# Two VectorE sums kept in PSUM: the state's sum and the product of kappa write over their own input

## The chip, the cores and the metric

The program runs on one core of one Trainium2 chip. The metric is the device time of one execution in microseconds (us); the time of a kernel is the median of its runs. Engines are named as in the profile: PE is TensorE, DVE is VectorE, ACT is ScalarE, POOL is GpSimd, SP issues most DMAs.

## The reference

One block of a network on 512 tokens of width 1024: a normed input goes through one wide projection; its columns feed a convolution branch (31 taps), an RWKV-7 branch with a state per head, and two gates; the branches are merged, projected, and a feed-forward network follows.

```
u = h @ w_in
u_conv, u_rwkv, u_gate = jnp.split(u, [2 * CONV_DIM, 2 * CONV_DIM + RWKV_COLS], axis=-1)
...
kk = (k * k_k).reshape(hs)
kk = kk / jnp.maximum(jnp.linalg.norm(kk, axis=-1, keepdims=True), 1e-12)
...
def step(S, inp):
    r_t, w_t, k_t, v_t, a_t, b_t = inp          # a_t = -kk
    Sa = jnp.einsum('bhij,bhj->bhi', S, a_t)
    S = S * w_t[:, :, None, :] + Sa[..., None] * b_t[:, :, None, :] + v_t[..., None] * k_t[:, :, None, :]
    y = jnp.einsum('bhij,bhj->bhi', S, r_t)
    return S, y
```

## The kernel before

Channels lie on the 128 partitions, the 512 tokens along the free axis. Every large product is cut into **dense blocks** of 128 output columns: `wload` fetches 128x8x128 weights (one DMA on SP's queue, two buffers "raw"), ACT rounds them to `wH` (L215), POOL computes the rest `wL = raw - wH` (L216), and `wmul` issues 24 matmuls of 128x512 (L223, L224, L225 in turn, eight times) into one of three PSUM buffers "mm". 52 such blocks stand ahead of the second half of group 3's solve, where they fill TensorE between the small products; behind the recurrence come dense blocks almost alone.

The RWKV heads are worked off in four **groups** g = 0 to 3 of four heads (two blocks b of 128 channels). The state's recurrence is cut into eight chunks of 64 tokens. For each group:

- `group_k` and `group_prep`: keys, decays and the factors of the chunks. In its part `decay_k`, once for each block, so 8 times, `bcast_rows` spreads the inverse norms over a PSUM tile `prn`; L628 multiplies it into BK, L630 makes `kkn = k * k_k * prn` and L631 makes AR from kkn and the decays `Pt`. `prn` is one of two PSUM buffers "misc", which the tiles post, g, bonus, mean and sW take in turn.
- `group_solve`: a triangular system, 31 steps on VectorE (L722 and L724 in each) between two transposes (L715 at the start, L730 at the end); `group_solve2` is its second half on TensorE and begins with the products sW (L748).
- `group_chain`: the eight chunks one after the other. A chunk's products go through one PSUM buffer "ch" on TensorE (L768 and L770, L777, L785); the new state is `S = (pn + S) * PC`, in L792 and L793 (L789 where there is no state yet, once in each group). The next chunk's L768 reads S. L792 and L793 are executed 24 times, six in each group.
- `group_post`: for each of the two blocks a transposition on TensorE (L830, tile post), its eviction on DVE (L831), a product g (L835) with weights `g2t` fetched on SP into one buffer, and its eviction (L836). `group_bonus` gives one more small product and its eviction (L702) to each block. These belong to group g and are laid among the work of g + 1.

The convolution's taps (L145, VectorE, `acc` in PSUM, which is written over) fill VectorE between the steps of the chain. In group 3 the convolution's norm is laid in: a product mean (L893) on TensorE, eight subtractions on POOL (L903), squares on ACT (L905), their sums (L188), a root (L198), its reciprocal on DVE (L199) and its broadcast on TensorE (tile rmsb, L183).

The order on each engine isn't written out: the program's text gives every instruction a priority, shifted by the numbers in the table `FORWARD` (`forward("chain", g)` and so on) and by `amid` and `issue_after`, and a scheduler takes at each point the instruction whose buffers and inputs it holds to be ready by its own costs. Which buffers a line uses is therefore part of what sets the order of all lines behind it.

Of the kernel before, what the change touches and what calls it, by code (L numbers as in the profile page):

```python
# [10 lines left out]
ALU = mybir.AluOpType  # L11
# [3 lines left out]
P = 128  # L15
# [3 lines left out]
C = 64  # L19
# [38 lines left out]
def tile_block(ctx: ExitStack, tc: tile.TileContext, xT, vec, cst, x0, w_ada, w_in, w2a2, g2w,  # L58
# [5 lines left out]
    dve, act, pool, pe = nc.vector, nc.scalar, nc.gpsimd, nc.tensor  # L64
    cnt = [0]

    def nm(s):
        cnt[0] += 1
        return f"{s}{cnt[0]}"
# [17 lines left out]
    def t2k(shape=(P, T), dt=F32, tag="t2k", bufs=9):  # L87
        home = sb if tag == "t2k" else pools["A2" if tag in A2 else "A"]
        return home.tile(list(shape), dt, name=nm(tag), tag=tag, bufs=bufs)
# [10 lines left out]
    def pmisc(shape=(P, T), name="misc"):  # L100
        return psum("misc", 2, shape, name)
# [4 lines left out]
    def V(name, j=0, w=1):  # L106
        o = VEC[name][0] + j
        return vt[:, o:o + w]
# [72 lines left out]
    def bcast_rows(dst, rows):  # L181
        for q in range(4):
            pe.matmul(dst[:, q * P:(q + 1) * P], e4[:, q, :], rows, start=True, stop=True)  # L183
# [49 lines left out]
    def after_dense():  # L233

        return tc.issue_after(last[0].ins)

    @contextmanager
    def amid(n, d=-1):

        with forward("amid", shift=False), tc.issue_after(dense_log[d][n].ins):  # L240
            yield
# [17 lines left out]
    def w_in_block(c0):  # L259
        return dense(w_in, 0, c0, hH, hL)  # L260

    def shifted(acc, dst, j, ahead=0):
        act.activation(dst, acc, AF.Copy, scale=mix1[:, j:j + 1])
        with forward("shift") if ahead else ExitStack():
            dve.scalar_tensor_tensor(dst[:, 1:T], acc[:, 0:T - 1], V("mix", j), dst[:, 1:T], ALU.mult, ALU.add)
# [268 lines left out]
    NB = 2  # L534
# [3 lines left out]
    def r3(ap):  # L538
        return ap.rearrange("p (c t) -> p c t", t=C)

    def atile(tag, shape, bufs=1):
        return pools["A2" if tag in A2 else "A"].tile(list(shape), F32, name=nm(tag), tag=tag, bufs=bufs)
# [50 lines left out]
    def group_prep(g, G):  # L593
        blocks = [g * NB + b for b in range(NB)]
        G.AR = atile("AR", (P, NB, NCH, 2 * C))
        G.UV = atile("UV", (P, NB, NCH, 2, C))
        G.bkT = atile("bkT", (P, NB, NCH, 2, C))
        G.G = atile("G", (P, NB, 2, NCH, P))
        G.PC = atile("PC", (P, NB, NCH), 2)
        Pts, Pis, BKs, kps = [], [], [], []  # L600
        for b, p in enumerate(blocks):
            cum = G.sg[b]
            dve.tensor_tensor_scan(cum, cmask, cum, 0.0, ALU.mult, ALU.add)
            Pt = atile("Pt", (P, NCH, C + 1), 2)
            pool.memset(Pt[:, :, 0:1], 1.0)
            with tc.issue_after(G.sqrt.ins):
                act.activation(Pt[:, :, 1:], r3(cum), AF.Exp, scale=-KAPPA)
            pool.tensor_copy(G.PC[:, b, :], Pt[:, :, C])
            Pi = t2k()
            with tc.issue_after(G.sqrt.ins):  # L610
                act.activation(Pi, cum, AF.Exp, scale=KAPPA)
            Pts.append(Pt)
            Pis.append(Pi)

        def decay_k(b, p):
            k, a = G.k[b], G.a[b]
            kP, kp = Pis[b], t2k()
            BK = atile("BK", (P, NCH, 3 * C), 2)
            pool.tensor_tensor(kP, k, Pis[b], ALU.mult)
            act.activation(kp, a, AF.Identity, scale=V("k_a", p), bias=ka1[:, p:p + 1])  # L620
            pool.tensor_tensor(BK[:, :, 0:C], r3(kP), r3(kp), ALU.mult)
            pool.tensor_copy(BK[64:128, :, 2 * C:3 * C], BK[64:128, :, 0:C])
            pool.tensor_tensor(kP, kP, a, ALU.mult)
            pool.tensor_tensor(kp, k, kp, ALU.mult)
            prn = pmisc(name="prn")
            with after_dense():
                bcast_rows(prn, G.rn[:, b, :])
            dve.scalar_tensor_tensor(BK[:, :, C:2 * C], r3(kP), V("k_k", p), r3(prn), ALU.mult, ALU.mult)  # L628
            kkn = t2k()
            dve.scalar_tensor_tensor(kkn, k, V("k_k", p), prn, ALU.mult, ALU.mult)  # L630
            dve.scalar_tensor_tensor(G.AR[:, b, :, 0:C], r3(kkn), -1.0, Pts[b][:, :, 0:C], ALU.mult, ALU.mult)  # L631
            BKs.append(BK)
            kps.append(kp)

        def load_r(b, p):
            r = t2k()
            shifted(w_in_block(R0 + p * P), r, p)
            return r

        def mul_r(b, p, r):  # L640
            dve.tensor_tensor(G.AR[:, b, :, C:2 * C], r3(r), Pts[b][:, :, 1:], ALU.mult)
            dve.scalar_tensor_tensor(r, r, V("r_k", p), kps[b], ALU.mult, ALU.mult)

        def load_v(b, p):
            v = t2k()
            shifted(w_in_block(R0 + 2 * D + p * P), v, 16 + p, 1)
            return v

        def products(b, p, r, v):
            BK = BKs[b]  # L650
            for cq in range(2):
                pt = pmisc((P, 4, 2, C), "bkt")
                for i in range(4):
                    pe.transpose(pt[:, i].rearrange("p e t -> p (e t)"), BK[:, cq * 4 + i, 0:2 * C], ident)
                cs = slice(cq * 4, cq * 4 + 4)
                act.copy(G.bkT[:, b, cs, 0, :], pt[:, :, 0, :])
                act.copy(G.bkT[0:64, b, cs, 1, :], pt[64:128, :, 1, :])
                act.copy(G.bkT[64:128, b, cs, 1, :], pt[0:64, :, 1, :])
            for cq in range(2):
                pgs = [pmisc((P, 4, P), "pG") for e in range(2)]  # L660
                for i in range(4):
                    c = cq * 4 + i
                    for e in range(2):
                        pe.matmul(pgs[e][:, i, :], BK[64 * e:64 * e + 64, c, C * e:C * e + 2 * C],  # L664
                                  G.AR[64 * e:64 * e + 64, b, c, :], start=True, stop=True)
                for e in range(2):
                    dve.tensor_tensor(G.G[:, b, e, cq * 4:cq * 4 + 4, :], pgs[e],  # L667
                                      gmask.unsqueeze(1).to_broadcast([P, 4, P]), ALU.mult)
            rH = t2k(dt=F32R)
            act.copy(rH, r)  # L670
            rL = t2k(dt=F32R)
            pool.tensor_tensor(rL, r, rH, ALU.subtract)
            G.bonus.append((rH, rL, v))
            pv = pmisc((P, 4, 2, C), "pv")
            for i in range(4):
                pe.transpose(pv[:, i].rearrange("p e t -> p (e t)"), v[:, i * P:(i + 1) * P], ident)
            for par in range(2):
                for e in range(2):
                    act.copy(G.UV[64 * e:64 * e + 64, b, par::2, e, :], pv[64 * par:64 * par + 64, :, e, :])

        rs, vs, G.bonus = [], [], []
        rs.append(load_r(0, blocks[0]))
        decay_k(0, blocks[0])
        mul_r(0, blocks[0], rs[0])
        vs.append(load_v(0, blocks[0]))
        decay_k(1, blocks[1])
        rs.append(load_r(1, blocks[1]))
        mul_r(1, blocks[1], rs[1])
        vs.append(load_v(1, blocks[1]))
        with amid(PREP_AT[0]):  # L690
            products(0, blocks[0], rs[0], vs[0])
        with (amid(PREP_AT[1]) if g < 2 else after_dense()):
            products(1, blocks[1], rs[1], vs[1])
        with after_dense():
            group_bonus(g, G, 0)
# [63 lines left out]
    def group_chain(G):  # L759
        Y = atile("Yt", (P, NCH // 2, NB, 2, C))  # L760
        S = None
        heads = [(b, e) for b in range(NB) for e in range(2)]
        for c in range(NCH):
# [17 lines left out]
            if c < NCH - 1:  # L781
                pn = psum("ch", 1, (P, NB, C))
                for b, e in heads:
                    lo = 64 * e
                    pe.matmul(pn[lo:lo + 64, b, :], G.bkT[:, b, c, e, :], G.UV[:, b, c, e, :], start=True, stop=True)  # L785
                Sn = atile("S", (P, NB, C), 2)
                pcb = G.PC[:, :, c].unsqueeze(2).to_broadcast([P, NB, C])
                if S is None:
                    dve.tensor_tensor(Sn, pn, pcb, ALU.mult)  # L789
                else:  # L790
                    sp = atile("sp", (P, NB, C))
                    dve.tensor_tensor(sp, pn, S, ALU.add)  # L792
                    dve.tensor_tensor(Sn, sp, pcb, ALU.mult)  # L793
            if c % 2 == 1:
                py = psum("Y", 1, (P, NB, 2, C))
                for b in range(NB):
# [7 lines left out]
            if c < NCH - 1:  # L804
                S = Sn
# [68 lines left out]
    with forward("k", 0):  # L874
        G = group_k(0)
    group_prep(0, G)
    for g in range(4):
# [38 lines left out]
        with forward("chain", g):  # L916
            Y = group_chain(G)
# [9 lines left out]
        G = Gn  # L927
# [244 lines left out]
```

## Time and profile before

| | |
|---|---|
| median of three runs | 1128.13 us (1125.83 to 1128.4) |
| the profiled execution | 1128.09 us, of which its span is 1126.3 us |
| mean granted TensorE clock | 0.973 of full speed |
| TensorE | 94% of the span, 6290 matmuls |
| VectorE | 67% of the span, 1133 instructions |
| ScalarE, GpSimd | 43%, 41% |

The profiled execution lies at the median of the runs. "Busy" adds up the time in which at least one instruction of an engine ran; the chain of work that ended last is 71% TensorE and 15% VectorE. [...]

### The profile page before, as it was taken

The numbers are of one execution on the slowest core, as the hardware profiler recorded it, in microseconds if no ns is written. First come the engines' busy times: TensorE is split into PE (matmuls) and PEld (weight loads), VectorE is DVE, ScalarE is ACT, GpSimd is POOL, SyncE is SP. The second block draws the span as 40 slices with busy tenths as digits, with TensorE's granted clock in tenths as the row PEclk, the third lists the DMA queues.
The fourth block names the chain that finished last, engine by engine and source line by source line (L and its number), as shares of the span: only waits on it lengthen the run. The fifth ranks groups of instructions, "written<-read, shape, count | busy, mean of one in ns | idle before, by whom it ended". The sixth has DMA issues, their size and how long they took to land.

```text
span 1126.3 us, 16021 instructions
## 1 busy us (share of the span) xinstructions
PE 1063.0 (94%) x6290; PEld 816.3 (72%) x6290; DVE 756.3 (67%) x1133; ACT 487.9 (43%) x794; POOL 460.5 (41%) x265
## 2 busy tenths in 40 slices
PE   6989899999999999999769999998999999999996
PEld 5766686677866677677445788876888888888885
DVE  5878887789878998679766757879413513512555
ACT  5557445547355654646363323335313312322431
POOL 4745442264424443443501244453444444444441
PEclk9989899899999999999968999999999999999999
DMA  9712242111521134022636689942333333333332
GB/s 318 228 42 84 61 127 76 52 57 59 179 87 52 39 105 153 20 67 84 214 118 215 217 281 298 290 131 57 94 96 103 101 94 94 94 94 96 104 99 77
DMA packets 188922, 136.73 MB, mean 121 GB/s; under 512 B 5424, under 2 KB 162480, under 8 KB 188848
## 3 DMA queue, kind: packets, MB, share of 16 engines
q1 hardware_dynamic: 188848, 135.73, 39.3%
q8 instruction: 49, 0.80, 0.3%
q14 instruction: 25, 0.20, 0.1%
HBM read 121.55 MB, written 14.16 MB: 120 GB/s over the span
## 4 chain that ended last, share of the span: by engine, by line
PE 71%; DVE 15%; ACT 5%; DMA 3%; POOL 3%; issue 2%; SPq 0%; DVEq 0%; ACTq 0%; POOLq 0%
PE mm L224 18%; PE mm L223 18%; PE mm L225 18%; DVE acc L145 2%; PE pG L664 2%; PE Y L802 1%; PE Y L800 1%; ACT wH L215 1%; POOL wL L216 1%; PE ch L768 1%; PE ch L777 1%; DVE t2k L251 1%; PE ch L785 1%; DVE t2k L1023 1%; POOL t2k L903 1%
## 5 line engine op out<-in xcount | busy, mean ns | idle before, releaser
L216 POOL TENSOR_TENSOR wL<-raw,wH 128x1024 fp32r<-128x1024 f32 x142 | 341.1, 2402 | 535.3 <-ACT wH L215 488.5
L225 PE MATMUL mm<-b,wL 128*128 128x512 f32 x720 | 289.6, 402 | 2.4 <-POOL wL L216 2.3
L224 PE MATMUL mm<-b,wH 128*128 128x512 f32 x720 | 289.0, 401 | 2.1 <-DVE b L1033 2.0
L223 PE MATMUL mm<-b,wH 128*128 128x512 f32 x720 | 289.7, 403 | 0.0
L215 ACT CAST wH<-raw 128x1024 fp32r<-128x1024 f32 x142 | 149.2, 1050 | 289.8 <-PE mm L224 246.3
L145 DVE SCALAR_TENSOR_TENSOR acc<-z,vt,acc 128x512 f32<-128x512 f32 x232 | 173.2, 746 | 1.6
L225 PEld LDWEIGHTS mm<-b,wL 128*128 128x128 f32 x720 | 135.9, 189 | 34.7 <-POOL wL L216 4.7
L224 PEld LDWEIGHTS mm<-b,wH 128*128 128x128 f32 x720 | 136.0, 189 | 33.2 <-DVE b L1033 3.4
L223 PEld LDWEIGHTS mm<-b,wH 128*128 128x128 f32 x720 | 136.0, 189 | 30.5 <-issue 3.2
L224 PE MATMUL mm<-g,wH 128*128 128x512 f32 x328 | 128.2, 391 | 1.1 <-DVE g L1025 0.9
L223 PE MATMUL mm<-g,wH 128*128 128x512 f32 x328 | 128.5, 392 | 0.0
L225 PE MATMUL mm<-g,wL 128*128 128x512 f32 x328 | 127.8, 390 | 0.0
L1023 DVE TENSOR_TENSOR t2k<-t2k 128x512 f32<-128x512 f32 x32 | 72.9, 2284 | 57.8 <-ACT t2k L1020 57.5
L1067 DVE SCALAR_TENSOR_TENSOR x<-mm,cols,x 128x512 f32<-128x512 f32 x31 | 23.3, 751 | 114.4 <-PE mm L225 114.4
L224 PEld LDWEIGHTS mm<-g,wH 128*128 128x128 f32 x328 | 61.6, 188 | 15.3 <-DVE g L1025 2.2
L223 PEld LDWEIGHTS mm<-g,wH 128*128 128x128 f32 x328 | 61.6, 188 | 14.0 <-ACT g L1024 1.2
L225 PEld LDWEIGHTS mm<-g,wL 128*128 128x128 f32 x328 | 61.6, 188 | 13.0 <-issue 0.2
L1024 ACT CAST g<-t2k 128x512 fp32r<-128x512 f32 x32 | 19.8, 621 | 72.6 <-DVE t2k L1023 72.6
L1025 DVE TENSOR_TENSOR g<-t2k,g 128x512 fp32r<-128x512 f32 x32 | 23.4, 736 | 19.9 <-ACT g L1024 19.9
L724 DVE TENSOR_TENSOR Y<-tm,Y 128x126 f32<-128x126 f32 (+22 forms) x124 | 31.8, 257 | 3.3
L664 PEld LDWEIGHTS pG<-AR,BK 64*128 64x128 f32 x256 | 24.7, 189 | 12.1 <-DVE G L667 6.3
L722 DVE TENSOR_TENSOR tm<-s,Y 128x126 f32<-128x126 f32 (+22 forms) x124 | 31.0, 250 | 3.1
(291 smaller groups left out, 1563.1 us busy)
## 6 DMA issues: line engine op xcount, KB each, us to landing
raw<-in_w_ff_dram SPq DMA_DIRECT2D x64, 512.0 KB, 4.0
raw<-in_w_in_dram SPq DMA_DIRECT2D x54, 512.0 KB, 3.7
adaw<-in_w_ada_dram SPq DMA_DIRECT2D x10, 1024.0 KB, 6.7
t2k<-gate SPq DMA_DIRECT2D x24, 256.0 KB, 3.9
adac<-in_w_ada_dram SPq DMA_DIRECT2D x24, 256.0 KB, 3.3
wa<-in_w_ada_dram SPq DMA_DIRECT2D x11, 512.0 KB, 5.8
gate<-cv SPq DMA_DIRECT2D x16, 256.0 KB, 2.9
raw<-in_w_pw_dram SPq DMA_DIRECT2D x8, 512.0 KB, 4.5
```

What stands on the lines that cost most here:

```text
L145: dve.scalar_tensor_tensor(dst if i == n - 1 else so_far, row, col, so_far, ALU.mult, ALU.add)
L215: act.copy(wH, raw)
L216: last_low[0] = pool.tensor_tensor(wL, raw, wH, ALU.subtract)
L223: steps.append(pe.matmul(acc, wH[:, kc, :], aH(kc), start=kc == 0, stop=False))
L224: steps.append(pe.matmul(acc, wH[:, kc, :], aL(kc), start=False, stop=False))
L225: steps.append(pe.matmul(acc, wL[:, kc, :], aH(kc), start=False, stop=kc == KC - 1))
L664: pe.matmul(pgs[e][:, i, :], BK[64 * e:64 * e + 64, c, C * e:C * e + 2 * C], G.AR[64 * e:64 * e + 64, b, c, :], start=True, stop=True)
L722: dve.tensor_tensor(tv, AT[:, s + 1:32, s].unsqueeze(2).to_broadcast([P, n, w]), X[:, s, 0:w].unsqueeze(1).to_broadcast([P, n, w]), ALU.mult)
L724: dve.tensor_tensor(X[:, s + 1:32, 0:w], tv, X[:, s + 1:32, 0:w], ALU.add)
L1023: dve.tensor_tensor(t, t, t, ALU.mult)
L1025: dve.tensor_tensor(rL(f), t, rH(f), ALU.subtract)
L1067: dve.scalar_tensor_tensor(x1(j), acc, ada[:, 40 + j:41 + j], x1(j), ALU.mult, ALU.add)
```

## The change

`kkn` and `sp` are no longer tiles in SBUF. L630 writes its product into `prn`, the PSUM tile that it reads, and the product AR reads it there; L792 writes the sum into `pn`, the PSUM tile that it reads, and L793 reads it there. As many instructions are issued as before, of the same sizes. In the program after, lines from L631 on count one less, lines from L792 on two less: L790 and L791 stand for L792 and L793, L629 and L630 for L630 and L631, L828 for L830, L829 for L831, L833 for L835, L834 for L836, L901 for L903, and L701 and L721 for L702 and L722.

```
             dve.scalar_tensor_tensor(BK[:, :, C:2 * C], r3(kP), V("k_k", p), r3(prn), ALU.mult, ALU.mult)
-            kkn = t2k()
-            dve.scalar_tensor_tensor(kkn, k, V("k_k", p), prn, ALU.mult, ALU.mult)
-            dve.scalar_tensor_tensor(G.AR[:, b, :, 0:C], r3(kkn), -1.0, Pts[b][:, :, 0:C], ALU.mult, ALU.mult)
+            dve.scalar_tensor_tensor(prn, k, V("k_k", p), prn, ALU.mult, ALU.mult)
+            dve.scalar_tensor_tensor(G.AR[:, b, :, 0:C], r3(prn), -1.0, Pts[b][:, :, 0:C], ALU.mult, ALU.mult)
...
                 else:
-                    sp = atile("sp", (P, NB, C))
-                    dve.tensor_tensor(sp, pn, S, ALU.add)
-                    dve.tensor_tensor(Sn, sp, pcb, ALU.mult)
+                    dve.tensor_tensor(pn, pn, S, ALU.add)
+                    dve.tensor_tensor(Sn, pn, pcb, ALU.mult)
```

Since a buffer of the nine "t2k" is taken 8 times less and "misc" is held longer, the scheduler gives another order: up to what runs at 118 us in the trace of before, and from what runs at 645 us on, the engines' orders are alike; between them they differ in many places. Three of them follow. Numbers behind a name (`S_1618`) count the program's tiles and differ between the two programs.

VectorE in group 0's chain, one step, before (`ch` is the tile pn, `z` and `acc` the convolution's):

```order
L780 COPY UV_765<-ch_1606 64x2x64
L145 SCALAR_TENSOR_TENSOR acc_1256<-z_1188,vt,acc_1256 128x512
L792 TENSOR_TENSOR sp_1619<-ch_1613,S_1591 128x128
L145 SCALAR_TENSOR_TENSOR acc_1256<-z_1188,vt,acc_1256 128x512
L793 TENSOR_TENSOR S_1618<-sp_1619,PC_768 128x128
```
and after:

```order
L779 COPY UV_765<-ch_1604 64x2x64
L145 SCALAR_TENSOR_TENSOR acc_1254<-z_1186,vt,acc_1254 128x512
L790 TENSOR_TENSOR ch_1611<-ch_1611,S_1589 128x128
L145 SCALAR_TENSOR_TENSOR acc_1254<-z_1186,vt,acc_1254 128x512
L791 TENSOR_TENSOR S_1616<-ch_1611,PC_768 128x128
```
The place in the row of instructions is the same; only the operands moved.

VectorE in the solve of group 1 (tile names `s`, `tm`, `Y`), where the evictions of group 0's post and g and of group 1's own bonus lie. Before, the first two stand ahead of the solve's start L715:

```order
L831 SCALAR_TENSOR_TENSOR vb_2308<-post_2310,vt,vb_2308 128x512
L145 SCALAR_TENSOR_TENSOR acc_1398<-z_1328,vt,acc_1398 128x512
L702 TENSOR_TENSOR t2k_2066<-bonus_2293,t2k_2066 128x512
L145 SCALAR_TENSOR_TENSOR acc_1398<-z_1328,vt,acc_1398 128x512
L715 STREAM_TRANSPOSE s_2345<-s_2336 128x1024
```
After, they stand in and behind the step whose tm has 128x133 elements, with those of g and of the second block close behind:

```order
L721 TENSOR_TENSOR tm_2339<-s_2335,Y_2337 128x133
L829 SCALAR_TENSOR_TENSOR vb_2298<-post_2300,vt,vb_2298 128x512
L723 TENSOR_TENSOR Y_2337<-tm_2339,Y_2337 128x19x7
L701 TENSOR_TENSOR t2k_2057<-bonus_2283,t2k_2057 128x512
L721 TENSOR_TENSOR tm_2339<-s_2335,Y_2337 128x126
L521 TENSOR_TENSOR z_2446<-mm_2454,cv_2444 128x512
L723 TENSOR_TENSOR Y_2337<-tm_2339,Y_2337 128x18x7
L521 TENSOR_TENSOR z_2553<-mm_2561,cv_2551 128x512
L721 TENSOR_TENSOR tm_2339<-s_2335,Y_2337 128x136
L834 SCALAR_TENSOR_TENSOR vb_2298<-vb_2298,vt,g_2308 128x512
L723 TENSOR_TENSOR Y_2337<-tm_2339,Y_2337 128x17x8
L829 SCALAR_TENSOR_TENSOR vb_2312<-post_2314,vt,vb_2312 128x512
```
L831 and L702 of the first block moved from ahead of the solve to its middle; the second block's and g's evictions stand in the middle in both programs.

TensorE at the same place, after (post and g are group 0's, bonus is group 1's; mm are dense blocks; 69 dense matmuls stand between the first two rows, 7 between the second post and the second g; before there were 6 from the first post to the first g, 3 more to the second post, and 108 from there to the second g):

```order
L828 MATMUL post_2300<-ct,Yt_1569 128x128 x4
...
L833 MATMUL g_2308<-sgx,g2t_2306 128x512
L828 MATMUL post_2314<-ct,Yt_1569 128x128 x4
L223 MATMUL mm_2663<-b_458,wH_2659 128x512
...
L833 MATMUL g_2322<-sgx,g2t_2320 128x512
L699 MATMUL bonus_2515<-t2k_2270,blkr 128x512
L700 MATMUL bonus_2515<-t2k_2272,blkr 128x512
```
Between the first post and the next group's first sW stand 134 dense matmuls, where 194 stood before; between the first sW of group 2 and that of group 3, 314 for 286; from there to the norm's mean 242 for 235; from mean to group 3's own sW 51 for 27. (Up to the first post it is 507 for 506, and up to group 3's sW 1248 in both.)

POOL at the norm in group 3, before (`t2k` are the convolution's rows):

```order
L216 TENSOR_TENSOR wL_5539<-raw_5536,wH_5538 128x1024
L903 TENSOR_TENSOR t2k_4969<-t2k_4969,t2k_4966 128x512
L903 TENSOR_TENSOR t2k_4971<-t2k_4971,t2k_4966 128x512
L903 TENSOR_TENSOR t2k_4973<-t2k_4973,t2k_4966 128x512
L903 TENSOR_TENSOR t2k_4975<-t2k_4975,t2k_4966 128x512
L903 TENSOR_TENSOR t2k_4977<-t2k_4977,t2k_4966 128x512
L903 TENSOR_TENSOR t2k_4979<-t2k_4979,t2k_4966 128x512
L216 TENSOR_TENSOR wL_5600<-raw_5597,wH_5599 128x1024
L903 TENSOR_TENSOR t2k_4981<-t2k_4981,t2k_4966 128x512
L903 TENSOR_TENSOR t2k_4983<-t2k_4983,t2k_4966 128x512
```
and after:

```order
L216 TENSOR_TENSOR wL_5433<-raw_5430,wH_5432 128x1024
L901 TENSOR_TENSOR t2k_4943<-t2k_4943,t2k_4940 128x512
L901 TENSOR_TENSOR t2k_4945<-t2k_4945,t2k_4940 128x512
L901 TENSOR_TENSOR t2k_4947<-t2k_4947,t2k_4940 128x512
L901 TENSOR_TENSOR t2k_4949<-t2k_4949,t2k_4940 128x512
L901 TENSOR_TENSOR t2k_4951<-t2k_4951,t2k_4940 128x512
L901 TENSOR_TENSOR t2k_4953<-t2k_4953,t2k_4940 128x512
L901 TENSOR_TENSOR t2k_4955<-t2k_4955,t2k_4940 128x512
L901 TENSOR_TENSOR t2k_4957<-t2k_4957,t2k_4940 128x512
L216 TENSOR_TENSOR wL_5507<-raw_5504,wH_5506 128x1024
```
The one L216 that stood between the sixth and the seventh subtraction stands behind the eighth.

## Rows read from the trace of the kernel before

**Rows 1.** Page, part 1: busy time and share of each engine

```profile
PE 1063.0 (94%) x6290; PEld 816.3 (72%) x6290; DVE 756.3 (67%) x1133; ACT 487.9 (43%) x794; POOL 460.5 (41%) x265
```


**Rows 2.** Groups of instructions, VectorE, 100 to 640 us: count, busy us, mean ns

```profile
L145 DVE SCALAR_TENSOR_TENSOR acc<-z,vt,acc 128x512 f32<-128x512 f32 x226 | 168.7, 746 | 1.4
...
L793 DVE TENSOR_TENSOR S<-sp,PC 128x128 f32<-128x128 f32 x24 | 14.6, 608 | 0.1
...
L792 DVE TENSOR_TENSOR sp<-ch,S 128x128 f32<-128x128 f32 x24 | 7.0, 292 | 30.4 <-PE ch L785 30.4
...
L630 DVE SCALAR_TENSOR_TENSOR t2k<-kk,vt,prn 128x512 f32<-128x512 f32 x8 | 5.9, 739 | 0.0
...
L789 DVE TENSOR_TENSOR S<-ch,PC 128x128 f32<-128x128 f32 x4 | 1.2, 290 | 1.9 <-PE ch L785 1.9
```


**Rows 3.** Instructions of L793: min/median/max ns; who waited (us, times)

```profile
L793 DVE TENSOR_TENSOR S<-sp,PC x24: 284/288/2420, 186.2 to 624.4; 128x128 f32<-128x128 f32 x24
...
  PE ch L768: 3.5, 3
```


**Rows 4.** Timeline of all engines from 206.5 us: start, duration, last the idle time

```profile
207.24 2.36 POOL L216 TENSOR_TENSOR wL<-raw,wH 128x1024 fp32r<-128x1024 f32 x1 [10.75 <-ACT wH L215]
207.33 2.42 DVE L793 TENSOR_TENSOR S<-sp,PC 128x128 f32<-128x128 f32 x1
...
209.89 0.49 PE L768 MATMUL ch<-S,AR 64*64 64x64 f32 x4 [1.00 <-DVE S L793]
```


**Rows 5.** Windows around two of these waits: busy us per engine, granted clock

```profile
200.00:208.00 8.00, 8.00 (x71) 5.05 (x67) 6.19 (x13) 3.35 (x8) 0.76 (x1) 1.00 0.06 18
208.00:218.00 10.00, 9.00 (x50) 5.14 (x50) 8.50 (x9) 5.84 (x11) 3.77 (x3) 0.66 0.25 79
...
610.00:620.00 10.00, 8.30 (x60) 5.33 (x61) 5.19 (x8) 2.39 (x8) 1.40 (x1) 0.66 0.65 212
```


**Rows 6.** Instructions of L631: min/median/max ns

```profile
L631 DVE SCALAR_TENSOR_TENSOR AR<-t2k,Pt x8: 679/689/2105, 112.3 to 511.9; 128x512 f32<-128x512 f32 x8
```


**Rows 7.** Instructions of L630: one line of who waited

```profile
  PEld pG L664: 0.8, 2
```


**Rows 8.** Timeline of TensorE from 273 us, first place

```profile
274.04 0.66 PE L830 MATMUL post<-ct,Yt 128*128 128x128 f32 x4
```


**Rows 9.** Timeline of VectorE, 274 to 326 us, in the second solve

```profile
299.73 0.29 DVE L722 TENSOR_TENSOR tm<-s,Y 128x133 f32<-128x133 f32 x1
...
303.61 0.75 DVE L836 SCALAR_TENSOR_TENSOR vb<-vb,vt,g 128x512 f32<-128x512 f32 x1 [2.73 <-PE g L835]
...
320.47 2.15 DVE L730 STREAM_TRANSPOSE s<-s 128x1024 f32<-128x1024 f32 x1
```


**Rows 10.** TensorE's waits: us in total, times, longest

```profile
PE sW L748 <- DVE s L730: 5.0, 3, 3.5
```


**Rows 11.** Timeline of TensorE around the second place, 546 to 573 us

```profile
546.70 1.02 PE L893 MATMUL mean<-csum,ones 128*128 128x512 f32 x2
...
548.02 0.40 PE L225 MATMUL mm<-b,wL 128*128 128x512 f32 x1
548.25 0.39 PE L223 MATMUL mm<-b,wH 128*128 128x512 f32 x1
...
572.95 1.92 PE L748 MATMUL sW<-s,G 32*32 32x32 f32 x64 [3.54 <-DVE s L730]
```


**Rows 12.** Timeline of GpSimd at the second place

```profile
551.75 7.44 POOL L903 TENSOR_TENSOR t2k<-t2k,t2k 128x512 f32<-128x512 f32 x6
559.16 2.34 POOL L216 TENSOR_TENSOR wL<-raw,wH 128x1024 fp32r<-128x1024 f32 x1
```


**Rows 13.** Page, part 5: the cast of weights on ScalarE, busy us, mean ns

```profile
L215 ACT CAST wH<-raw 128x1024 fp32r<-128x1024 f32 x142 | 149.2, 1050 | 289.8 <-PE mm L224 246.3
```


**Rows 14.** Windows of the second place

```profile
546.00:573.00 27.00, 14.71 (x108) 8.77 (x108) 16.98 (x50) 13.43 (x19) 14.56 (x10) 0.78 0.59 188
568.00:573.00 5.00, 1.46 (x10) 1.20 (x11) 4.09 (x5) 3.12 (x4) 0.00 (x0) 0.50 0.00 0
```


## The prediction

> **What bounds the kernel now.** I read the page first: TensorE is busy in 94% of the span, VectorE in 67%, POOL in 41% [rows 1]. So VectorE's own time is worth nothing by itself; a faster VectorE instruction counts only where TensorE stands still for it, and what one more TensorE instruction costs is its issue interval, where nothing else is late. Then the groups of VectorE over the stretch in which the recurrence runs [rows 2]. L792 and L793 do the same sort of work on the same 128x128, yet L792 takes 292 ns on the mean and L793 608. L792 has one input in PSUM, L793 both in SBUF. The view of L793 alone says that this is no steady price: the median is 288 ns, the longest 2420 [rows 3]. Busy 14.6 us less 24 x 0.288 leaves 7.7 us of excess. The timeline at the worst one shows its cause as far as a trace can: L793 starts 0.09 us behind a POOL L216 and ends at 209.75, 0.15 us after that L216 ended [rows 4]. Eight of the 24 are long in this way, each ending where a POOL instruction ends, while no L792 is, though eight or more of them ran beside one too.
>
> What that costs the path is in the list of who waited: TensorE's L768, 3.5 us in three waits [rows 3]; the one at 209.89 lasted 1.00 us [rows 4]. There is a second bill behind it. In the windows the granted clock is 1.00 in the 8 us ahead of that wait, and 0.66 in the 10 us from 208 on; the 10 us from 610, which hold the longest of the three waits, have 0.66 too [rows 5]. A stretch at 0.66 gives away (1 - 0.66) x 10 = 3.4 us of full-speed time.
>
> **The change, part by part.**
>
> *The chain's sum (24 times).* L792 writes PSUM instead of SBUF. Its nearest price is the tap L145, 746 ns with output in PSUM, against L630, 739 ns with output in SBUF, both on 512 columns [rows 2]: under 10 ns, taken as 0. L793 becomes the form of L789, which has PSUM and SBUF inputs and takes 290 ns [rows 2] for 288. That is 0.05 us over all 24, nothing. What goes is the holding up by POOL, if L793 behaves as L792 and L789 do: TensorE's 3.5 us of waits, between 0 (if POOL still holds it) and 7.7 (if all of the excess lay on the path). I take **-3.5**, since the list of waits says who stood still. The two half-clock stretches go with the waits that precede them: **-6.8**, between 0 and -6.8.
>
> [...]
>
> *The product of kappa (8 times).* AR's median is 689 ns, its longest 2105 [rows 6]. From PSUM I price it as the other 512-column products that read PSUM, 739 to 746 [rows 2], so +0.05 x 8 = 0.4 us of VectorE time, which lies beside TensorE's dense matmuls. Nobody is listed as waiting for AR, though one of its long ones lies on the chain that ended last; in the new order that one stands later anyway. Taken: 0, bounds -1.4 (2.105 - 0.689) and +0.4.
>
> *The buffer that prn holds.* `prn` is now free only behind AR, 1 to 25 VectorE instructions later than before, and post, g, bonus and sW queue for the same two buffers. L630 already held up TensorE there, for 0.8 us at its longest entry [rows 7], 1.5 us over all. I take **+1.0**, bounds 0 and +2.
>
> *The order.* This is the larger unknown. Dense matmuls issue 0.233 us apart (548.02, 548.25) [rows 11], which prices each that is moved.
>
> First place, from group 0's post to the first sW of the next group. Post starts at 274.04 [rows 8]; with 0.45 for it and 69 x 0.233 = 16.1 for the dense matmuls behind it, TensorE comes to the first g at 290.6. The g needs a "misc" buffer, and so the eviction of post, which now stands in the step of 128x133. That step lies at 299.73 [rows 9]; it comes two evictions of some 0.7 us earlier, since these no longer stand ahead, and the eviction takes 0.75 itself: done at about 299.4. **TensorE is held for some 8.7 us.** Queued behind it are the second post, g and bonus, 65 dense matmuls and sW. VectorE, on the other hand, no longer waits 2.73 us for g [rows 9]. sW follows VectorE's last transpose, as its three waits in group 1 to 3 show [rows 10]; that transpose ends at 320.47 + 2.15 = 322.62, so sW comes **-2.7** earlier (0 if VectorE waits elsewhere), near 319.9. TensorE's own work behind the hold is 65 x 0.233 and some 1.8 us of small products, 16.9 us, so it would be ready at 316.3; the second g's weights are fetched on SP behind a store that waits for the bonus's eviction, which may eat a us of that. A half-clock stretch behind the hold, 3.4 us as in [rows 5], nearly fits into what is left: **+0.5**, bounds 0 and 3.4.
>
> But 60 dense matmuls that stood ahead of this sW now come later: 28 between the sW of group 2 and that of group 3 counted as [rows 10] does (**+6.5**), 7 to the norm's mean (**+1.6**), and 24 behind it. The first two stretches have no idle TensorE to speak of, so I take them whole; lower bound 0.
>
> Second place, the norm: from mean at 546.70 to sW at 572.95 TensorE is busy only 14.71 us of 27 [rows 11, 14], so 24 x 0.233 = 5.6 us find room. What ends the stretch is the chain POOL subtractions, ACT squares, root, broadcast, end of the solve. In it the L216 at 559.16, 2.34 us [rows 12], moves behind the subtractions; in exchange one more cast of weights on ACT, 1.05 us on the mean [rows 13], comes ahead of the end: **-1.3**, upper bound +5.6 if the block isn't hidden.
>
> Sum: -3.5 - 6.8 + 1.0 + 0.5 - 2.7 + 6.5 + 1.6 - 1.3 = -4.7. From the profiled execution's 1128.09 us, which is the median of the runs within 0.1 us, that is **1123.4 us**. All lower bounds together give 1128.1 - 7.7 - 6.8 - 1.4 - 2.7 - 1.3 = 1108, all upper ones 1128.1 + 0.4 + 2 + 3.4 + 6.5 + 1.6 + 5.6 = 1148.
>
> **The rivals.** A measurement of this kernel tells about 0.3%, 3.4 us, from no change.
>
> *The reorder eats the gain.* The half clock from 610 on isn't the wait's doing alone: even in that window TensorE was busy only 8.30 of 10 us [rows 5]. If it stays (+3.4) and the norm gives back nothing (+1.3), the time is 1128.1: no change. For it: the last slices of the recurrence are TensorE's loosest. Against it: the same 0.66 followed a wait of 1.00 us at 208, where TensorE was full before.
>
> *Slower: the block behind mean runs at half clock.* In the last 5 us ahead of group 3's sW the granted clock is 0.50 [rows 14]. If the 24 matmuls are issued there, ahead of the sums of squares and the broadcast that the chain needs, they cost 24 x 0.466 = 11.2 us and nothing hides them: 1123.4 + 1.3 + 11.2 = 1135.9. It decides from the point at which mean to sW takes over 33 us (26.25 - 1.3, and the 8.1 us from 1123.4 to 1131.5). For it: TensorE works in order, and the block stands ahead of the broadcast. Against it: 12.3 idle us in that stretch.
>
> *The change doesn't do what it says.* If an instruction with one input in PSUM is still held by POOL, the 10.3 us of direct gain are gone and the order's part stays: 1133.7. L792's 24 short ones speak against it [rows 2].
>
> **How the numbers follow.** Forecast 0.48 (its own range 1115 to 1124.7), the reorder eats the gain 0.28, slower by the block at half clock 0.19, no effect 0.05. The predicted time is the forecast's, 1123.4. The range 1112 to 1136 leaves out the forecast's far end and the upper half of the slower case, some 0.15. Faster by over 0.3% has 0.48, within 0.3% 0.28, slower 0.24.
>
> **What would show it.** Right: the new L793 has a longest duration under 0.5 us, no wait of TensorE names the state S, and the windows from 208 and from 610 show 1.00. The g (L833 after) waits some 8 us for the eviction of post, and sW of group 1's solve lies within 3 us of the old place. Mean to sW takes some 25 us. The prediction is wrong if the clock falls behind the 8.7 us hold and stays down into the next chain, if TensorE waits longer for misc buffers than 2 us in all, or if the reorder puts new waits into the chains of groups 1 and 2, which I priced only by counts of matmuls.

## The result

The changed kernel takes 1136.36 us (median of four runs, 1133.86 to 1137.79), the kernel before 1128.27 us in the runs beside it: a ratio of 1.0069, 95% interval 1.0041 to 1.0097, so some 8 us slower. The forecast was 1123.4 us in a range of 1112 to 1136. The profiled execution of the changed kernel, from which the rows below are read, is the fastest of its four (1133.86 us); that of before lies at its median (1128.09 us). Ratios here and below are taken over all runs of both kernels and are not quotients of the medians.

The operands did what was expected of them. The groups of VectorE between 100 and 640 us of the changed kernel, in the columns of [rows 2]:

```profile
L145 DVE SCALAR_TENSOR_TENSOR acc<-z,vt,acc 128x512 f32<-128x512 f32 x224 | 167.3, 747 | 1.5 <-ACT acc L143 0.2
...
L790 DVE TENSOR_TENSOR ch<-ch,S 128x128 f32<-128x128 f32 x24 | 7.2, 300 | 25.3 <-PE ch L784 25.3
...
L791 DVE TENSOR_TENSOR S<-ch,PC 128x128 f32<-128x128 f32 x24 | 6.8, 284 | 0.1
L629 DVE SCALAR_TENSOR_TENSOR prn<-kk,vt,prn 128x512 f32<-128x512 f32 x8 | 6.0, 744 | 0.0
...
L630 DVE SCALAR_TENSOR_TENSOR AR<-prn,Pt 128x512 f32<-128x512 f32 x8 | 5.5, 682 | 0.3 <-PE Y L798 0.3
```
and AR before, in the same columns:

```profile
L631 DVE SCALAR_TENSOR_TENSOR AR<-t2k,Pt 128x512 f32<-128x512 f32 x8 | 9.1, 1140 | 0.4 <-PE Y L800 0.4
```
The state's product (L791) has a mean of 284 ns where it had 608, the product AR (L630) 682 where it had 1140. VectorE's busy time falls from 756.3 to 738.9 us, and no wait of TensorE names the state S. What TensorE waits for instead is in its list of waits (us in total, times, longest):

```profile
PE g L833 <- DVE vb L829: 8.5, 1, 8.5
PE mm L225 <- POOL wL L216: 8.0, 4, 4.1
...
PE sW L747 <- DVE s L729: 3.3, 3, 1.6
...
PE post L828 <- DVE Yt L820: 2.1, 2, 1.6
```
The second row had 2.3 us before. All but 1.3 us of it lies ahead of group 0's post, which the changed kernel reaches earlier in spite of it.

Where the time went is read from stretches between the same products in both kernels: from group 0's post to the sW of group 1's solve, on to the sW of group 2, to the norm's mean, to the sW of group 3. (Groups count from 0; what the text on the change calls the way from the sW of group 2 to that of group 3, with 314 dense matmuls for 286, is the second of these stretches.) The windows before:

```profile
274.04:322.68 48.64, 47.48 (x209) 38.17 (x208) 42.60 (x104) 19.15 (x25) 21.59 (x11) 1.00 0.47 146
322.68:440.62 117.94, 114.95 (x891) 83.24 (x891) 103.17 (x193) 64.78 (x120) 45.50 (x31) 1.00 0.27 83
440.62:546.70 106.08, 103.87 (x841) 73.48 (x840) 85.29 (x146) 61.10 (x115) 39.72 (x25) 1.00 0.24 74
546.70:572.95 26.25, 13.96 (x103) 8.18 (x102) 16.23 (x49) 13.43 (x19) 14.56 (x10) 0.78 0.58 188
```
and after:

```profile
269.48:316.29 46.81, 36.73 (x149) 28.63 (x147) 41.42 (x103) 13.25 (x18) 16.90 (x9) 0.89 0.38 123
316.29:446.96 130.67, 127.37 (x918) 91.30 (x918) 100.66 (x195) 66.03 (x122) 48.89 (x32) 0.95 0.26 78
446.96:556.23 109.27, 106.96 (x847) 75.69 (x847) 84.20 (x147) 61.03 (x115) 39.51 (x25) 1.00 0.24 73
556.23:581.77 25.54, 18.36 (x127) 11.56 (x127) 16.51 (x48) 16.08 (x22) 17.01 (x11) 0.97 0.65 205
```
The first number behind the colon is the length, then TensorE's busy time; the granted clock is the number behind POOL's. The changed kernel reaches the first post 4.6 us earlier. It loses 12.7 us from the sW of group 1 to that of group 2 (130.67 for 117.94), with 3 us of idle TensorE in both: the clock is 0.95 there for 1.00, so by an estimate from it (1 - 0.95) x 130.67 = 6.5 us went to half clock, and 28 more dense matmuls at 0.233 us are about the rest (6.5). Another 3.2 us go on the way to mean. The 8.5 us hold lies in the first of the stretches and cost no time there (46.81 for 48.64).

The hold in the timeline of VectorE, in the solve of group 1:

```profile
293.30 0.28 DVE L721 TENSOR_TENSOR tm<-s,Y 128x133 f32<-128x133 f32 x1
293.50 0.74 DVE L829 SCALAR_TENSOR_TENSOR vb<-post,vt,vb 128x512 f32<-128x512 f32 x1
...
295.15 0.68 DVE L521 TENSOR_TENSOR z<-mm,cv 128x512 f32<-128x512 f32 x1
...
295.94 0.68 DVE L521 TENSOR_TENSOR z<-mm,cv 128x512 f32<-128x512 f32 x1
```
and of TensorE:

```profile
285.38 0.39 PE L225 MATMUL mm<-b,wL 128*128 128x512 f32 x1
294.29 2.08 PE L833 MATMUL g<-sgx,g2t 128*128 128x512 f32 x2 [8.53 <-DVE vb L829]
296.16 1.06 PE L828 MATMUL post<-ct,Yt 128*128 128x128 f32 x4
```
TensorE issues its last dense matmul at 285.38 and then nothing until 294.29. The granted clock around it and around the sW at 316.29:

```profile
286.00:290.00 4.00, 0.00 (x0) 0.00 (x0) 4.00 (x10) 0.66 (x1) 2.35 (x1) 0.99 0.20 60
290.00:294.00 4.00, 0.00 (x0) 0.00 (x0) 4.00 (x10) 0.00 (x0) 0.55 (x1) 0.50 0.45 131
...
298.00:302.00 4.00, 4.00 (x13) 2.86 (x12) 2.30 (x8) 0.00 (x0) 0.00 (x0) 0.73 0.49 170
302.00:306.00 4.00, 4.00 (x20) 3.27 (x19) 3.66 (x13) 0.42 (x1) 0.00 (x0) 1.00 0.63 213
316.00:320.00 4.00, 3.71 (x71) 2.74 (x71) 3.93 (x5) 2.28 (x4) 0.00 (x0) 0.65 0.35 104
320.00:324.00 4.00, 4.00 (x67) 2.75 (x67) 2.45 (x4) 2.22 (x5) 0.00 (x0) 0.50 0.00 0
...
328.00:332.00 4.00, 4.00 (x20) 2.51 (x20) 1.17 (x4) 1.91 (x3) 2.01 (x1) 0.64 0.00 0
332.00:336.00 4.00, 4.00 (x37) 2.44 (x37) 3.49 (x8) 1.12 (x4) 0.35 (x1) 1.00 0.56 162
```
It goes to 0.50 in the idle stretch, is back before 302, and falls a second time behind the sW, from some 317 to 331 us, where TensorE is busy all the time and the lower clock is paid for: dense matmuls start 0.43 us apart there (328.18, 328.60, 329.03), and 0.23 us apart ahead of the hold (284.70, 284.92, 285.15). In windows of 1 us, from 284 to 306 and from 314 to 336, the clock is 1.00 in 18 and 0.50 in 22 of the 44, and 0.58 to 0.94 in the four in which it changes.

### The profile page after: what moved, and what is told of

It reads as the page before. It is cut to its first block, busy times and chain, and to the rows that moved or that the text cites. A ratio compares the mean times of both kernels' runs of the same rounds, so it can differ in the third digit from the quotient of the medians.

```text
span 1131.6 us, 16039 instructions
## 1 busy us (share of the span) xinstructions
PE 1063.1 (94%) x6290; PEld 814.8 (72%) x6290; DVE 738.9 (65%) x1133; ACT 487.1 (43%) x795; POOL 460.0 (41%) x265
## 4 chain that ended last, share of the span: by engine, by line
PE 39%; DVE 5%; DMA 3%; ACT 2%; POOL 1%; issue 1%; SPq 0%; DVEq 0%; ACTq 0%
PE mm L224 12%; PE mm L225 12%; PE mm L223 12%; DVE t2k L1021 1%; ACT wH L215 1%; DVE b L1031 1%; DVE acc L145 1%; DMA raw<-in_w_o_dram 1%; DMA adaw<-in_w_ada_dram 1%; DMA adac<-in_w_ada_dram 1%; DMA g2t<-in_g2w_dram 1%; POOL t2k L901 0%; PE mm L1079 0%; DVE t2k L979 0%; POOL wL L216 0%
## 5 line engine op out<-in xcount | busy, mean ns | idle before, releaser
L216 POOL TENSOR_TENSOR wL<-raw,wH 128x1024 fp32r<-128x1024 f32 x142 | 342.8, 2414 | 546.2 <-ACT wH L215 535.5
L721 DVE TENSOR_TENSOR tm<-s,Y 128x126 f32<-128x126 f32 (+22 forms) x124 | 31.0, 250 | 3.3
```

What stands on the lines that cost most here:

```text
L216: last_low[0] = pool.tensor_tensor(wL, raw, wH, ALU.subtract)
L721: dve.tensor_tensor(tv, AT[:, s + 1:32, s].unsqueeze(2).to_broadcast([P, n, w]), X[:, s, 0:w].unsqueeze(1).to_broadcast([P, n, w]), ALU.mult)
```

## The experiments

Theory A: the operands gain about 10 us, and the new order loses more. The order turns on one VectorE instruction, the first convolution eviction of group 1 (L521, which frees the "mm" buffer of a dense block): ahead of the solve before, inside it after. Theory B, the main rival: the new operands hold PSUM buffers longer and that costs. The prediction's own account is a third: the eviction of post (L829) holds TensorE.

**One eviction moved, both ways.** To the kernel before, e1 adds only

```
+            if s == 12:
+                G.step12 = ins                    # the solve's second instruction of step 12
...
         acc_a = w_in_block(p * P)
+        with tc.issue_after(G.step12.ins):        # for p == 4 alone
             dve.tensor_tensor(z[:, PAD:], acc_a, sz, ALU.mult)
```

> The operands are those of before; only the first convolution eviction of group 1 (L521, first of the two) is put behind step 12 of the solve. Theory A (this one eviction sets the order): TensorE stands 8 us or more in the solve of group 1, 59 dense matmuls come behind its sW, and the kernel takes some 13 us more than before, 1141. Theory B (the new operands hold their PSUM buffers longer, and that costs): no operand changed, so 1128.

Measured 1140.92 us against 1127.77, ratio 1.0097 (1.0063 to 1.0131). Its dense matmuls stand almost exactly as after's: 135 from the first post to the sW of group 1, 312 to the next. TensorE is held for 7.81 us, by name at the second g:

```profile
297.93 2.07 PE L841 MATMUL g<-sgx,g2t 128*128 128x512 f32 x2 [7.81 <-DVE vb L842]
```
No operand changed, so theory B can't account for it. e1 loses in a second place too, where the changed kernel loses little: from the sW of group 2 to mean it takes 116.2 us, at a clock of 0.96, for 106.1 before and 109.3 after.

To the kernel after, e2 adds only

```
+        with tc.high_priority(offset=300):        # for p == 4 alone
             dve.tensor_tensor(z[:, PAD:], acc_a, sz, ALU.mult)
```

> The operands are those of after; only the first convolution eviction of group 1 is given a higher priority, so that it stands ahead of the solve as it did before. Theory A: the hold of 8.5 us and the half clock behind sW go, and what is left is the gain of the operands, 8 to 10 us under before: 1118 to 1122. Theory B: within 2 us of after, 1134 to 1138. The prediction's own account (the eviction of post holds TensorE) gives 1134 to 1138 too, since that eviction stays inside the solve.

Measured 1130.69 us, ratio 1.0032 (1.0000 to 1.0064) against before, 5.7 us under after and 9 to 13 over what theory A said. The interval overlaps that of after (1.0041 to 1.0097), so the time alone doesn't settle what the eviction costs in the changed kernel. The hold is gone though the eviction of post still stands inside the solve, at the time that it has in after: 119 dense matmuls stand between the first post and the first g, 69 in after's order. TensorE reaches g at 296.99 without a wait, and in the profiled execution the clock stays at 1.00 behind the sW. VectorE's eviction, TensorE's g and the windows:

```profile
293.54 0.74 DVE L833 SCALAR_TENSOR_TENSOR vb<-post,vt,vb 128x512 f32<-128x512 f32 x1
296.99 1.02 PE L837 MATMUL g<-sgx,g2t 128*128 128x512 f32 x2
318.47:441.71 123.24, 121.42 (x911) 87.52 (x911) 98.35 (x194) 66.99 (x123) 47.40 (x33) 1.00 0.28 85
548.39:575.38 26.99, 11.31 (x88) 6.06 (x88) 18.13 (x56) 12.11 (x17) 12.16 (x9) 0.62 0.54 185
```
So the eviction of post doesn't make the hold by itself, which is what the prediction's account needs. The last row is where the gain probably went in that order: from mean to sW TensorE is busy 11.31 us of 26.99, where it was 13.96 of 26.25 before. 21 more dense matmuls stand between the sW of groups 1 and 2 than before (307 for 286, and the stretch takes 123.24 us), and only 13 for 27 are left to fill the norm.

One profile doesn't stand for e2, though. Of its twelve executions on one chip six took 1127.2 to 1128.5 us at a mean granted clock of 0.975 to 0.979, the profiled one among them, and six 1132.8 to 1139.7 us at 0.965 to 0.972; the median lies between. The difference in clock, 0.0095 on the mean or some 10.7 us of an execution, is as large as that in time (8.8 us). Where in the other six the clock fell is on no trace.

**One half of the change alone.** e3 keeps the state's sum in PSUM and kkn in SBUF; e4 the other way round.

> Only the state's sum stays in PSUM; kkn is in SBUF as before. In its order the evictions of post and bonus stand ahead of the solve, as before, but the convolution's eviction stands inside it, as after. Theory A: the waits on S and their half clock are gone (8 us), the order costs as in after, so about after's time, 1134 to 1138, with the hold on another instruction. The prediction's account (post's eviction is what holds): no hold, 1122 to 1126.

> Only kappa's product is in PSUM; the state's sum is as before. Theory A: order as bad as after's and no gain in the chains: 8 us over after, 1142 to 1146. If the kappa part costs nothing by itself: 1128.

e3: 1136.40 us, ratio 1.0054 (1.0022 to 1.0086); e4: 1137.35 us, 1.0078 (1.0054 to 1.0103). e3's eleven executions spread from 1125.25 to 1138.74 us, and the profiled one is the longest. Each half alone brings an order with the late L521. In e3 the evictions of post and bonus stand ahead of the solve, as before the change, and TensorE is held all the same, at the next g:

```profile
291.20 2.08 PE L834 MATMUL g<-sgx,g2t 128*128 128x512 f32 x2 [7.37 <-DVE vb L835]
```
e4 came out 5 to 9 us under theory A's number. The half clock behind 208 isn't there: from the sW of group 0 to its post it takes 98.05 us at a clock of 1.00, where before took 102.87 at 0.97. That the long state products cost TensorE less in this order is the author's estimate from these two stretches; no view of them shows it.

**Operands and order crossed.** Four programs, in which either the operands of L792 and L793 or the order of all engines is exchanged. The order is held by edges between neighbours on an engine, which fix the issue order:

```
+    for k in ORDER:          # per engine, the other program's order
...
+            tc.add_manual_dep(traced[k], traced[prev].name,
+                              mybir.DependencyInfo(mybir.DependencyClass.NoSync, mybir.DependencyReason.DATA), reason="order")
```

> Only the state's sum is in PSUM (kkn as before), and every engine's instructions are held to the order of before, so that nothing but the operands of L792 and L793 differs. Theory A (the operands gain, the order loses): the waits on S and the half clock behind them go, at least the 4.4 us of group 0's chain and 3.5 us of group 3's, 1118 to 1121. Rival: the gain is swallowed by what VectorE and TensorE wait for next, 1126 to 1128.

> The operands are those of before, every engine's order is that of the run with only the state's sum in PSUM. Theory A: the order's loss without the operands' gain, 1140 to 1145. If the operands gain nothing by themselves: 1136, as with the sum in PSUM in this order.

| | order of before | order of e3 |
|---|---|---|
| sum in SBUF | before: 1128.56 us | e6: 1143.91, ratio 1.0129 (1.0092 to 1.0166) |
| sum in PSUM | e5: 1118.06, ratio 0.9907 (0.9873 to 0.9940) | e3: 1136.40, ratio 1.0054 (1.0022 to 1.0086) |

In the traces the row of instructions of TensorE, VectorE, ScalarE and GpSimd is the same in e5 as in before, and in e6 as in e3. The operands gain 10.5 us in the order of before and 7.5 us in the other; the order costs 15.4 us with the old operands and 18.3 with the new. (e3 ran beside another set of runs of before, whose median was 1127.77.) This is the order of e3, not that of after: like e1 it takes 118.3 us (e6: 117.2) from the sW of group 2 to mean, where after takes 109.3. e5 is faster than both kernels. In e5, where the state's product is L792, it lies between 281 and 292 ns (min, median, max); in e6 it is L793, is held up again, and TensorE waits for it. The views of these instructions, e5 first:

```profile
L792 DVE TENSOR_TENSOR S<-ch,PC x24: 281/285/292, 183.4 to 619.8; 128x128 f32<-128x128 f32 x24
```
The same view of e6:

```profile
L793 DVE TENSOR_TENSOR S<-sp,PC x24: 284/290/2432, 188.1 to 636.3; 128x128 f32<-128x128 f32 x24
...
  PE ch L768: 2.4, 3
```
**A filler for the norm.** e7 is e2 with the third number of the table's row "post" (group 2's) set from 0 to 40; this is what its expectation means by the shift of group 2's post.

> As the run of after's operands with the early convolution eviction, but the shift of group 2's post in the table is 40 for 0-third entry 0, which puts 24 instead of 13 dense matmuls between the norm's mean and group 3's sW. If that filler is what the early eviction's run lost, 11 x 0.233 = 2.6 us and no more than 5 us less: 1124 to 1128. If not: 1128 to 1131 as there.

A miss: 1141.06 us, ratio 1.0101 (1.0050 to 1.0153). The 24 matmuls stand behind mean as wanted, but the same number also moved group 2's evictions to the start of group 3's solve, and the sW waits 12.92 us for VectorE. So it doesn't tell whether the filler was what e2 lost:

```profile
587.66 1.92 PE L751 MATMUL sW<-s,G 32*32 32x32 f32 x64 [12.92 <-DVE s L733]
```
**The same programs again.** Is the half clock a property of the program?

> The same program as the run with the sum in PSUM and the order of before, executed again. There 1123.67 us in the profiled execution (the other six 1116 to 1119) went with 8.7 us lost to half clock between the sW of groups 1 and 2. If the half clock behind sW is a matter of the execution: about 1118 us and no such stretch, or 1123 with one. If it belongs to the program: the stretch is there again, whatever the time.

> The changed kernel again. Its hold of TensorE by 8.5 us in the solve of group 1 comes again, since the order sets it. If the half clock behind that solve (6.5 us lost in the first profile) follows from the hold, it comes again too; if it is a matter of the execution, it may be absent, and the time is then some 6 us lower or has lost it elsewhere.

> The kernel before again. The long state products (2.1 to 2.4 us, three waits of TensorE, 3.5 us) should come again, at the same steps, if the order sets where POOL meets them; the half clock behind the waits at 208 and 610 (3.4 us lost each) too, if it follows from the waits. Time 1126 to 1130.

They took 1121.68, 1136.14 and 1126.59 us, one execution each, and before took 1125.75 beside them. e8 fits neither of its two cases: the stretch is absent, and the time is still 3.6 us over the median of e5. The window from the sW of group 1 to that of group 2 in e5, then the same program in e8 and the changed kernel again in e9:

```profile
315.91:440.84 124.93, 122.22 (x891) 87.81 (x891) 102.10 (x193) 64.76 (x120) 45.42 (x31) 0.93 0.26 78
```
e8:

```profile
318.39:436.36 117.97, 114.76 (x890) 83.30 (x890) 101.92 (x193) 64.81 (x120) 45.47 (x31) 1.00 0.27 83
```
e9:

```profile
315.21:445.34 130.13, 127.06 (x918) 91.31 (x919) 100.66 (x195) 66.03 (x122) 48.86 (x32) 0.95 0.26 79
```
One program, 0.93 and then 1.00: 7 us between two executions of e5's program, which ran on two chips; e2's twelve executions show a spread of this size on one. After's second execution repeats its first (0.95, and a hold of 8.5 us). Over all profiles, each of the six with a hold (after twice, e1, e3, e4, e6) lost 6.5 us or more to half clock in this stretch; of the six without, before, e2 and e8 lost nothing, e10 3.6, e5 8.7 and e7 9.1. In the six with a hold the clock falls behind the sW: 0.50 from 320 to 324 in after, 0.66 from 320 to 330 in e1, 0.61 from 310 to 320 in e3, 0.50 from 320 to 330 in e4 and e6, and in e9 dense matmuls start 0.43 us apart at 317 and 322, for 0.23 at 313. Of the others it does so in e5 (0.50 from 320 to 330) and e7 (0.59 from 320 to 340). So a hold isn't needed for it. In e10 the long state product came again at the same step, with the same wait:

```profile
204.91 2.37 POOL L216 TENSOR_TENSOR wL<-raw,wH 128x1024 fp32r<-128x1024 f32 x1 [10.74 <-ACT wH L215]
205.00 2.43 DVE L793 TENSOR_TENSOR S<-sp,PC 128x128 f32<-128x128 f32 x1
...
207.57 0.34 PE L768 MATMUL ch<-S,AR 64*64 64x64 f32 x4 [1.01 <-DVE S L793]
```
but the clock did not follow this time, while it fell again at the later place:

```profile
205.00:215.00 10.00, 8.99 (x81) 5.17 (x81) 9.58 (x12) 6.90 (x13) 4.48 (x3) 1.00 0.25 79
608.00:618.00 10.00, 8.88 (x74) 5.82 (x74) 4.62 (x8) 2.59 (x8) 0.82 (x1) 0.66 0.66 210
```

## Why the prediction was wrong

*The operands' gain: right in mechanism, its sum in part by luck.* No L791 is longer than 292 ns, and the sum written in place costs 300 ns for 292 (L790), under the 10 ns allowed for. (Seven, not eight, of the 24 old products were long: the eighth in length took 300 ns.) The -10.3 us stand against -10.5 us in e5, where nothing else changed, but the interval of e5's ratio runs from -7 to -14 us. The profiles show the gain in two places: from the sW of group 0 to its post 98.9 us in e5 and 99.0 in e8, for 102.9 in before and 100.1 in e10, and from the sW of group 3 to its post 66.8 and 66.3 for 71.5 twice; together 6 to 9 us. The -6.8 us for two half-clock stretches were too sure: the stretch behind 610 is lost in both executions of before and is gone in e5 and in the changed kernel (their windows of that place are below), while the one behind 208 was there in one execution of before and absent in the other, with the same wait of 1.0 us ahead of it. A wait of that length precedes a fall of the clock in some executions and not in others. The window of e5, then that of the changed kernel:

```profile
610.00:620.00 10.00, 10.00 (x104) 6.58 (x105) 5.24 (x11) 3.59 (x11) 1.50 (x1) 1.00 0.80 269
608.00:618.00 10.00, 10.00 (x104) 6.74 (x103) 5.16 (x11) 4.86 (x11) 4.14 (x2) 1.00 0.75 243
```

*AR: right to count as nothing*, though its price was wrong: 682 ns from PSUM, less than the 689 from SBUF, not 739 to 746.

*The longer hold on prn: +1.0 predicted, nothing seen.* After has 0.4 us of weight loads waiting for L629, and no wait of TensorE for AR. But it doesn't go with the order of before: there AR of group 2's second block (388.68 us) stands on VectorE behind four evictions of the products pG (L667, from 383.65 on), which the program makes in pairs that take both "misc" buffers. With `prn` held until AR, each would wait for the other. So no run has both halves of the change in the order of before; this is argued from the row of instructions, not shown.

*The order: the step that failed.* "A half-clock stretch behind the hold, 3.4 us as in [rows 5], nearly fits into what is left: +0.5, bounds 0 and 3.4." The hold came as worked out, 8.5 us for 8.7, and cost nothing in its own stretch, as said. But the clock fell twice, and the second stretch lies behind the sW, where TensorE sets the pace: 6.5 us in both executions, beyond the bound given. It is the largest single miss, 6.0 of the some 10 us between the forecast and the profiled execution; the text came near it under what would make it wrong, though the clock did not stay down but came back and fell again. Next, 7 matmuls more to mean were priced at 1.6 us and that stretch took 3.2 more. Its idle time is the same (2.3 us for 2.2), its busy time 3.1 us longer; what the other half of that is stays open. A wait that the counts of matmuls did not price is in the stretch ahead of it: 1.55 us for the post of group 1 (part of the 2.1 us in the list of waits), where before had 0.2; other waits there are shorter, so that its idle time hardly grew. The other terms of the order held: sW -1.8 for -2.7, the 28 matmuls +6.5, mean to sW -0.7 for -1.3.

*The cause of the hold was named in its last link alone.* The g waits for the eviction of post, as the prediction said. But e2 shows that post's eviction can stay inside the solve without a hold, e3 and e1 that it can stand ahead of it and the hold stays. What all held orders share, and e2 and before do not, is L521 inside the solve. Two dense blocks wait there in "mm" buffers (the two L521 of the order after), so TensorE has one buffer of three for everything behind; it runs dry and stands at whichever small product is next in its row: behind 69 dense matmuls from the first post on in after, 70 in e1, 68 in e3 and e6, 71 in e4, while e2 has 119 and before 117 ahead of the small product at that place. That the third buffer is what runs out is argued from the order; that moving the one eviction makes and removes the hold is shown.

*The rivals.* "The reorder eats the gain" came true in its name, not in its terms: it asked for the half clock from 610 to stay and the norm to give back nothing, and the first is gone and the norm gave 0.7 us. The slower rival, the block at half clock behind mean, did not come true, and that its 1135.9 us lie near the measured time is luck: mean to sW took 25.54 us with 51 dense matmuls in it, and the clock there was 0.97 where it had been 0.78. That POOL still holds the product is excluded by the 292 ns. That an order with the late eviction loses is thus shown (e1, e5, e6). In the changed kernel the half clock behind the solve and the dense matmuls that moved there are 6.5 us each; what makes the clock fall in one execution and not in another stays open.

## What to carry to other kernels

Where a scheduler sets the order, cost a change of operands and its new order apart, and if the order is the worse part, hold the old one: here the larger half of the change is worth -10.5 us with the order held, and the whole change comes out at +8 us without. A wait names the instruction at the head of the row; ask what work ran out ahead of it, and which eviction keeps the buffers of that work. Where the clock fell in one execution and not in the next, as behind the solve here, one profile doesn't give its price: put the whole of such a stretch (7 us here) into the range, and compare several executions.

## What was not expected of the hardware

VectorE's products paid nothing for a source in PSUM: 284 ns on the mean for 128 columns (288 at the median from SBUF), 682 for 512 columns (689 at the median from SBUF). With both inputs in SBUF the state's product of before ran beside a GpSimd instruction in 13 of 24 cases; seven of these took 0.88 to 2.42 us, each ending 0.14 or 0.15 us behind a GpSimd instruction, and the longest in e6 and e10 took 2.43 us. With one input in PSUM it took at most 0.292 us, in 24 of 24 instructions, in two orders (after, e5), though 11 of them in after ran beside a GpSimd instruction. The stretch from the sW of group 1 to that of group 2 differed between two executions of one program by 7 us (124.93 at a clock of 0.93 in e5, 117.97 at 1.00 in e8), with a wait of 1.14 and 1.12 us at the sW ahead of it.
